# A fused decoder block on one core: three stages' weight pieces in a new order, and the weight fetches pinned in program order

## The chip, the core and the metric

The kernel runs on one core of a Trainium2 chip. The time is the device time of one execution in microseconds (us), and the median of several executions is what counts. A profile is one further execution, recorded by the hardware profiler; its own time is given beside its span. The engines are called as in the profile: PE is TensorE (PEld its weight loads), DVE is VectorE, ACT is ScalarE, POOL is GpSimd, and SP is the queue that issues most DMAs.

## What is computed

A decoder block for 256 tokens and a model width of 2048: a mixer with two branches, an output projection, a feed-forward network and a final norm, all in float32.

```python
def hybrid_mixer(h, w_in, ...):
    proj = h @ w_in                       # 16400 columns
    q, k, v, g_out, gk_low, gate_b, gate_c, xc, merge_a, merge_b = split(proj)
    log_g = log_sigmoid(gk_low @ w_gk_up + b_gk_up) / 16
    o = rmsnorm(gla_chunked(q, k, v, log_g))        # 4 heads, chunks of 64
    y_a = o * silu(g_out)
    y_b = gate_b * causal_depthwise_conv(gate_c * xc, conv_w)     # 3 taps
    return (sigmoid(merge_a) * y_a + sigmoid(merge_b) * y_b) @ w_out

h = x + hybrid_mixer(rmsnorm(x), ...)
h = h + (silu(rmsnorm(h) @ w_gate) * (rmsnorm(h) @ w_up)) @ w_down   # 5632 hidden
out = rmsnorm(h)
```

## The kernel before, in words

**Products and pieces.** All weights are read once, in pieces of 128 x 1024 values (512 KB). A piece is fetched by SP into a tile `raw` (five buffers), ACT makes its rounded upper half `hi` (`high`, L266, six buffers) and DVE the remainder `lo` (`low`, L271, five buffers). The activations are held as two such halves too. A product is three matmuls, hi by lo, lo by hi and hi by hi (`mm3`, L375 to L377). A plain piece of 512 columns has two blocks of 128 rows, for each of which it is multiplied with both halves of the tokens: twelve matmuls of 512 columns.

**Pairs.** Some column groups are computed in pairs by a scheme with seven products in place of eight (`sevens`, `seven_list`, `mixed`). A pair has 28 pieces of six matmuls. Twenty of them come in four quads q = 0 to 3, each in the order 11, t1, t3, t2, t4; then come the eight pieces 21 and 22. Sixteen pieces, the t's, are sums or differences of weight pieces that DVE makes first (`sum_of`): 11 is fetched into a tile `y` (one buffer), t1 fetches `x` (two buffers) and makes y + x into a raw tile (L287); t3, t2 and t4 then change x in place (L293), t3 and t4 with a fetched piece of their own, t2 with y. So a quad fetches y, x and two raw pieces, all by `fetch` (L260), and plain pieces are fetched at L323.

**The order.** `stream_list` writes out the order of all pieces: first k0, q0, v0; then `heads_list`, with the pair Values 2 and 3 (v2, v3) among plain pieces of other keys, queries and values; then `gates_list`, with four pairs gc and xc (the two factors ahead of the convolution) among plain pieces of the gates g, gb, ma and mb; then the output projection wo; then `hidden_list`, with pairs fg and fu among plain pieces of fg, fu and the down projection dn; then the last dn. `mixed` lays plain pieces into the gaps of a pair: one after each t, then one after each 21 and 22, and so on.

`run` takes one piece after the other. Before piece n is used, `take` has loaded all up to n + 5 (LOOK), so fetch, cast, sum and split of a piece are written down five pieces ahead of its matmuls; `low` lags one piece behind `high`. After each piece the count of ticks goes up by one, and work that was put off until then (`later`, `at`) is written down: the attention, the tables of the decay (`tables_within`, L786 and L787, at tick 22), the scores, the convolution, the merges and the transposes.

**Who orders the instructions.** The framework takes each engine's instructions in the order of the program but may move one ahead of others when it is ready sooner by its own estimate. `pin` (`keep_in_program_order`) forbids it: the instruction stays behind the one written before it on the same engine. Before the change only the convolution's and the merges' products on DVE and a few on ACT are pinned. The fetches on SP are not.

**Gates, convolution, merge.** When a gc pair is done, `conv` (one tick later) copies its product u, shifted by one and two rows, through POOL's DMA queue (L976 to L981); five pinned DVE products (L989) follow from tick CONV_AT = 12 on. `gate` finishes a plain gate; after mb it sets the merge (L994, L995) for the later of the next tick and `merge_at`, which the pair has set. The merged block is transposed (trb, L631) for wo. PSUM has eight banks; plain groups borrow theirs from the list `lent` (three banks), from which transposes, scores (sc_ps, L851) and attention products (o_ps) take one at a time.

Of the kernel before, what the change touches and what calls it, by code (L numbers as in the profile page):

```python
# [17 lines left out]
NT = T // P  # L18
D = 2048
KC = D // P  # L20
# [23 lines left out]
def plan():  # L44
# [26 lines left out]
DOWN = (WHOLE, WHOLE, WHOLE, ((0, 512), (512, 512), (1024, 512), (1536, 256), (1792, 256)))  # L71


GATES = (
    (("gc0", "xc0"), ("g1", "gb0", "mb0")),
    (("gc1", "xc1"), ("ma1", "gb1", "mb1")),
    (("gc2", "xc2"), ("g2", "ma2", "gb2")),
    (("gc3", "xc3"), ("mb2", "g3", "ma3")),
    (None, ("gb3", "mb3")),
)  # L80

# [22 lines left out]
    return [(pair, e) for e in out + list(twos)]  # L104


def mixed(pair, eights, late=None):


    if pair is None:  # L110
        return eights
    sevens = seven_list(pair)
    sums = ("t1", "t3", "t2", "t4")
    gaps = [0] * len(sevens)
    rest = len(eights)

    def deal(some, most):
        nonlocal rest
        for n, (_, e) in enumerate(sevens):
            if e[0] in some and most > 0 and rest > 0:  # L120
                gaps[n] += 1
                rest -= 1
                most -= 1

    if late is not None:
        deal(("21", "22"), late)
        while rest > 0:
            deal(sums + ("11",), rest)
    while rest > 0:
        for some in (sums, ("21", "22")):  # L130
            deal(some, rest)
    out, put = [], 0
    for e, n in zip(sevens, gaps):
        out += [e] + eights[put:put + n]
        put += n
    return out


def gates_list():
    return [e for pair, keys in GATES  # L140
            for e in mixed(pair, [(key, k) for key in keys for k in range(0, KC, 2)])]


def heads_list():


    step = {"k": 4, "q": 4, "v": 2, "g": 2, "m": 2}
    plain = [(key, k) for key in ("k1", "q1", "v1", "k2", "q2", "k3", "q3", "g0") for k in range(0, KC, step[key[0]])]
    n = plain.index(("v1", 8))
    gate = [("ma0", k) for k in range(0, KC, 2)]  # L150

    return plain[:n] + mixed(("v2", "v3"), plain[n:-1], 4) + gate[:4] + plain[-1:] + gate[4:]


def block_of(key):
# [52 lines left out]
def block_kernel(ctx, tc, x, xt, cols_in, gkw_in, gku_in, gnw, conv_w, finw, w_in, w_out, w_gu, w_dn, out):  # L208
    nc = tc.nc
    pin = tc.keep_in_program_order  # L210
    mats = {"w_in": w_in, "w_out": w_out, "w_gu": w_gu, "w_dn": w_dn}
# [40 lines left out]
    count = {"loaded": 0, "used": 0, "tick": 0}  # L252
# [4 lines left out]
    def fetch(key, k0, pool=wraw, tag="raw"):  # L257
        mat, j, n, w = index[(key, k0)]
        raw = pool.tile([P, n, w], F32, tag=tag, name=tag, bufs={"x": 2, "y": 1}.get(tag))
        nc.sync.dma_start(raw, mats[mat][j].rearrange("p (k c) -> p k c", c=w))  # L260
        return raw

    def high(raw, piece, a=0, b=None):
# [32 lines left out]
    def load_piece():  # L296


        i = count["loaded"]
        count["loaded"] += 1  # L300
        if i < len(stream):
            key, k0 = stream[i]
            if isinstance(k0, tuple):
                n, w = 2, 512
                raw = sum_of(key, *k0)
                step = n
            else:
                mat, j, n, w = index[(key, k0)]
                raw = wraw.tile([P, n, w], F32, tag="raw", name="raw")

                step = n // 2 if i < 2 else n
            piece = [whi.tile([P, n, w], F32R, tag="hi", name="hi"), None, n]
            if isinstance(k0, tuple):
                high(raw, piece)
                halfway.append((raw, piece, key, k0))
            else:
                if i < 2:
                    piece[1] = wlo.tile([P, n, w], F32R, tag="lo", name="lo")
                for a in range(0, n, step):
# [3 lines left out]
                    nc.sync.dma_start(  # L323
                        raw[:, a:b, :], mats[mat][j, :, a * w:b * w].rearrange("p (k c) -> p k c", c=w))
# [16 lines left out]
    def later(delay, fn):  # L341

        pending.append((count["tick"] + delay, fn))
# [461 lines left out]
    def at(tick, fn):  # L805
        later(tick - count["tick"], fn)
# [57 lines left out]
    o = {}  # L864
# [101 lines left out]
    us, ya, sb, merge_at = {}, {}, {}, {}  # L966

    def conv(i):
        u = us[i]
        u1 = ew.tile([P, NT, 512], F32, tag="u1", name="u1")  # L970
        u2 = ew.tile([P, NT, 512], F32, tag="u2", name="u2")
        taps = ew.tile([P, 3, 512], F32, tag="taps", name="taps")
        nc.gpsimd.dma_start(taps, conv_w[:, :, i * 512:(i + 1) * 512].to_broadcast([P, 3, 512]))
        nc.gpsimd.memset(u1[0:1, 0, :], 0.0)
        nc.gpsimd.memset(u2[0:2, 0, :], 0.0)
        nc.gpsimd.dma_start(u1[1:113, :, :], u[0:112, :, :])  # L976
        nc.gpsimd.dma_start(u2[2:114, :, :], u[0:112, :, :])
        nc.gpsimd.dma_start(u1[113:128, :, :], u[112:127, :, :])
        nc.gpsimd.dma_start(u2[114:128, :, :], u[112:126, :, :])
        nc.gpsimd.dma_start(u1[0:1, 1, :], u[127:128, 0, :])  # L980
        nc.gpsimd.dma_start(u2[0:2, 1, :], u[126:128, 0, :])  # L981

        def taps_of(j):
            return taps[:, j:j + 1, :].to_broadcast([P, NT, 512])

        for n, (dst, src, by, op) in enumerate(((u1, u1, 1, ALU.mult), (u2, u2, 0, ALU.mult), (u, u, 2, ALU.mult),
                                                (u1, u1, u2, ALU.add), (u, u, u1, ALU.add))):
            by = taps_of(by) if isinstance(by, int) else by
            later(CONV_AT + n, lambda d=dst, s=src, y=by, o=op: pin(nc.vector.tensor_tensor(out=d, in0=s, in1=y, op=o)))  # L989

    def merge(i, ts):

# [9 lines left out]
    def gated(dst, ps):  # L1002

        for t in range(NT):
            nc.scalar.activation(ps[t], ps[t], AF.Sigmoid, scale=r1[:, t:t + 1])
            nc.vector.tensor_tensor(out=dst[:, t, :], in0=dst[:, t, :], in1=ps[t], op=ALU.mult)

    def gate(key):
        i = int(key[-1])

        def done(ps):
            if key[:-1] == "g":
                ya[i] = ew.tile([P, NT, 512], F32, tag=f"ya{i % 2}", name="ya")
                for t in range(NT):
                    nc.scalar.activation(ya[i][:, t, :], ps[t], AF.Silu, scale=r1[:, t:t + 1])
# [12 lines left out]
        return done  # L1028

    def gate_pair(pair):  # L1030
        i = int(pair[0][-1])

        def second(t):
            to = us if pair[0][:-1] == "gc" else sb
            if i not in to:
                to[i] = ew.tile([P, NT, 512], F32, tag="u" if to is us else "sb", name="u" if to is us else "sb")
            return to[i][:, t, :]

        def done(t, one, two):
# [12 lines left out]

        return second, done
# [194 lines left out]
    for e in order:  # L1248
        key, k0 = e
        n = int(key.split("_")[1])  # L1250
# [80 lines left out]
```

## Time and profile before

| | before |
|---|---|
| time, median of 3 runs | 1507.15 us (1506.55 to 1508.85) |
| profiled execution: time | 1508.41 us |
| profiled execution: span | 1506.5 us |
| PE busy | 1487.1 us, 99% of the span |
| DVE busy | 1312.4 us, 87% |
| ACT busy | 874.6 us, 58% |
| read from HBM | 355.23 MB, 237 GB/s over the span |

How the views are read: a row of the timeline has the start and the length of an instruction in us, its engine, line and operation, then out<-in by the program's names; behind it in brackets stands how long the engine was idle before it and what ended that. A row of the waits has engine, tile and line of the one that waited, what it waited for, and the total in us, the number of times and the longest. A row of the windows has the stretch and its length, then the busy time and the number of instructions of PE, PEld, DVE, ACT and POOL (or of the one engine asked for), the granted clock of TensorE as a share of full speed, the DMA engines' busy share and GB/s. A row of the groups has the number of instructions, then busy us and mean ns of one, then the idle time before them. A row of the DMA issues has the queue, the number, the size of each and the median us from issue to landing. A matmul of 512 columns is shown with some 390 ns although the next one begins after 225; a stall shown as idle is therefore a little shorter than the time lost between two starts.

### The profile page before, as it was taken

What the parts mean: (1) busy time and instruction counts of PE and PEld (TensorE: products, weight loads), DVE (VectorE), ACT (ScalarE), POOL (GpSimd) and SP (SyncE); (2) the same over time, 40 slices, a digit from 0 to 9 for tenths busy, and PEclk for the clock granted to TensorE, in tenths of its full rate; (3) what the DMA queues carried; (4) which work ended last, traced back from release to release, by engine and by line L of the source; (5) the groups of instructions that cost most, each with busy time, mean ns of one, the idle gap of its engine ahead of it and who ended that gap; (6) DMA issues with size and microseconds to landing.
All of it is one profiled execution on the core that took longest, in us unless ns stands there. A gap on an engine that the chain in (4) does not pass through costs nothing.

```text
span 1506.5 us, 19393 instructions
## 1 busy us (share of the span) xinstructions
PE 1487.1 (99%) x7040; PEld 1240.7 (82%) x7040; DVE 1312.4 (87%) x1316; ACT 874.6 (58%) x990; POOL 33.0 (2%) x60
## 2 busy tenths in 40 slices
PE   9999999999999999999999999999999999999997
PEld 8979988888888788788888888888888788888887
DVE  7998878978989889976688999999999999989975
ACT  7855566655564564564566755655565556555553
POOL 0010000000001001000000000000000000000000
PEclk9999999999999999999999999999999999999999
DMA  9656677787786786787676777777877778777682
GB/s 351 216 168 193 199 238 229 238 269 234 247 294 211 242 291 225 263 296 216 210 220 220 237 257 249 250 247 232 270 240 240 258 258 273 239 265 232 229 303 87
DMA packets 101280, 362.78 MB, mean 241 GB/s; under 512 B 11620, under 2 KB 11748, under 8 KB 101056
## 3 DMA queue, kind: packets, MB, share of 16 engines
q1 hardware_dynamic: 97808, 350.92, 70.1%
q0 software_dynamic: 2800, 8.89, 2.1%
q10 hardware_dynamic: 576, 1.72, 0.3%
q8 instruction: 55, 0.90, 0.2%
q14 instruction: 41, 0.34, 0.1%
HBM read 355.23 MB, written 2.10 MB: 237 GB/s over the span
## 4 chain that ended last, share of the span: by engine, by line
PE 91%; DVE 5%; issue 1%; DMA 1%; ACT 1%; SPq 0%; DVEq 0%; ACTq 0%
PE fg L375 8%; PE fg L377 8%; PE fg L376 8%; PE dn L375 5%; PE dn L377 5%; PE dn L376 5%; PE gc L375 3%; PE gc L377 3%; PE gc L376 3%; PE wo L375 2%; PE mb L377 2%; PE mb L375 2%; PE mb L376 2%; DVE lo L271 2%; PE wo L376 2%; PE wo L377 2%
## 5 line engine op out<-in xcount | busy, mean ns | idle before, releaser
L271 DVE TENSOR_TENSOR lo<-raw,hi 128x1024 fp32r<-128x1024 f32 (+1 forms) x502 | 607.1, 1217 | 91.9 <-ACT hi L266 22.3
L266 ACT CAST hi<-raw 128x1024 fp32r<-128x1024 f32 (+1 forms) x502 | 520.0, 1047 | 242.4 <-PE mb L377 28.6
L266 ACT CAST hi<-x 128x1024 fp32r<-128x1024 f32 x156 | 164.2, 1053 | 287.4 <-DVE x L293 217.3
L271 DVE TENSOR_TENSOR lo<-x,hi 128x1024 fp32r<-128x1024 f32 x156 | 190.8, 1223 | 42.5 <-ACT hi L266 30.9
L375 PE MATMUL dn<-lo,acth 128*128 128x512 f32 (+1 forms) x368 | 140.7, 382 | 1.7 <-DVE h L1186 1.0
L377 PE MATMUL dn<-hi,acth 128*128 128x512 f32 (+1 forms) x368 | 139.9, 380 | 0.0
L376 PE MATMUL dn<-hi,actl 128*128 128x512 f32 (+1 forms) x368 | 139.8, 380 | 0.0
L293 DVE TENSOR_TENSOR x<-x,raw 128x1024 f32<-128x1024 f32 x104 | 126.8, 1219 | 12.6 <-DMA raw<-in_w_in_dram 7.8
L375 PE MATMUL fg<-lo,hh 128*128 128x512 f32 x288 | 112.4, 390 | 0.0
L377 PE MATMUL fg<-hi,hh 128*128 128x512 f32 x288 | 112.2, 390 | 0.0
L376 PE MATMUL fg<-hi,hl 128*128 128x512 f32 x288 | 112.1, 389 | 0.0
L375 PE MATMUL fg<-lo,sh 128*128 128x512 f32 x256 | 101.0, 395 | 0.0
L376 PE MATMUL fg<-hi,sl 128*128 128x512 f32 x256 | 99.9, 390 | 0.0
L377 PE MATMUL fg<-hi,sh 128*128 128x512 f32 x256 | 99.8, 390 | 0.0
L375 PEld LDWEIGHTS dn<-lo,acth 128*128 128x128 f32 x368 | 69.2, 188 | 15.8 <-DVE h L1186 1.8
L377 PEld LDWEIGHTS dn<-hi,acth 128*128 128x128 f32 x368 | 69.2, 188 | 13.3
L376 PEld LDWEIGHTS dn<-hi,actl 128*128 128x128 f32 x368 | 69.2, 188 | 12.9
L271 DVE TENSOR_TENSOR lo<-y,hi 128x1024 fp32r<-128x1024 f32 x52 | 63.4, 1219 | 4.1 <-PE g L375 1.4
L287 DVE TENSOR_TENSOR raw<-y,x 128x1024 f32<-128x1024 f32 x52 | 63.3, 1218 | 2.8 <-DMA y<-in_w_gu_dram 2.5
L293 DVE TENSOR_TENSOR x<-x,y 128x1024 f32<-128x1024 f32 x52 | 63.5, 1220 | 0.7
L375 PEld LDWEIGHTS fg<-lo,hh 128*128 128x128 f32 x288 | 54.1, 188 | 11.7 <-DVE lo L271 0.5
L377 PEld LDWEIGHTS fg<-hi,hh 128*128 128x128 f32 x288 | 54.1, 188 | 11.2
(268 smaller groups left out, 3059.4 us busy)
## 6 DMA issues: line engine op xcount, KB each, us to landing
raw<-in_w_in_dram SPq DMA_DIRECT2D x254, 512.0 KB, 4.6
raw<-in_w_gu_dram SPq DMA_DIRECT2D x176, 512.0 KB, 4.4
raw<-in_w_dn_dram SPq DMA_DIRECT2D x88, 512.0 KB, 4.5
x<-in_w_gu_dram SPq DMA_DIRECT2D x32, 512.0 KB, 5.1
y<-in_w_gu_dram SPq DMA_DIRECT2D x32, 512.0 KB, 3.9
raw<-in_w_out_dram SPq DMA_DIRECT2D x32, 512.0 KB, 3.9
y<-in_w_in_dram SPq DMA_DIRECT2D x20, 512.0 KB, 4.0
x<-in_w_in_dram SPq DMA_DIRECT2D x20, 512.0 KB, 5.1
```

The lines of the kernel that those rows point to most:

```text
L266: nc.scalar.copy(hi[:, ks, :], raw[:, ks, :])
L271: nc.vector.tensor_tensor(out=lo[:, ks, :], in0=raw[:, ks, :], in1=hi[:, ks, :].bitcast(F32), op=ALU.subtract)
L287: nc.vector.tensor_tensor(out=raw, in0=y, in1=held["x"], op=ALU.add)
L293: nc.vector.tensor_tensor(out=x, in0=x, in1=other, op=ALU.add)
L375: nc.tensor.matmul(ps, lhsT=sh, rhs=ml, start=first, stop=False, skip_group_check=onto)
L376: nc.tensor.matmul(ps, lhsT=sl, rhs=mh, start=False, stop=False, skip_group_check=onto)
L377: nc.tensor.matmul(ps, lhsT=sh, rhs=mh, start=False, stop=last, skip_group_check=onto)
```

## The change

It has three parts, and helpers for them.

1. Heads: the gaps of the pair v2 and v3 are written out as a list, HEADS. It has 25 plain pieces inside the pair in place of 27, so the pair begins two plain pieces later: behind v1's sixth piece, not its fourth. In its first quad the plain pieces behind 11, t1, t3, t2 and t4 are 2, 2, 1, 2, 1, where they were 2, 2, 2, 1, 1. At the end 1, 1, 0, 1, 0, 1, 0, 0 stand behind the 21 and 22 pieces, where it was 1, 1, 1, 1, 0, 0, 0, 0, and t1 and t4 of the last quad have none.
2. Fetches: both places that fetch weights (L260 and L323) are pinned.
3. Gates: the 14 plain gates are one list, of which each pair takes 25 pieces (before: 24, three whole gates). The second of two plain pieces comes behind t1 of the first quad. Behind the last pair 12 plain pieces are left (before 16). The last convolution's products start 7 ticks after it, not 12. As a gate can now end before or after its pair, `merge_when` is called by both, and the second call sets the merge.

```diff
-GATES = (
-    (("gc0", "xc0"), ("g1", "gb0", "mb0")),
-    (("gc1", "xc1"), ("ma1", "gb1", "mb1")),
-    (("gc2", "xc2"), ("g2", "ma2", "gb2")),
-    (("gc3", "xc3"), ("mb2", "g3", "ma3")),
-    (None, ("gb3", "mb3")),
-)
+GATES = (("gc0", "xc0"), ("gc1", "xc1"), ("gc2", "xc2"), ("gc3", "xc3"))
+GATES_PLAIN = ("g1", "gb0", "mb0", "ma1", "gb1", "mb1", "g2", "ma2", "gb2", "mb2", "g3", "ma3", "gb3", "mb3")
+GATES_EACH = 25
+
+HEADS = (2, 2, 1, 2, 1, 1, 1, 1, 1, 1, 1, 1, 1, 1, 1, 1, 0, 1, 1, 0, 1, 1, 0, 1, 0, 1, 0, 0)
...
-def mixed(pair, eights, late=None):
+def mixed(pair, eights, gaps=None):
...
+    if gaps is None:
+        gaps = [0] * len(sevens)
+        rest = len(eights)
         while rest > 0:
-            deal(sums + ("11",), rest)
-    while rest > 0:
-        for some in (sums, ("21", "22")):
-            deal(some, rest)
+            for some in (sums, ("21", "22")):
+                for n, (_, e) in enumerate(sevens):
+                    if e[0] in some and rest > 0:
+                        gaps[n] += 1
+                        rest -= 1
...
 def gates_list():
-    return [e for pair, keys in GATES
-            for e in mixed(pair, [(key, k) for key in keys for k in range(0, KC, 2)])]
+    plain = [(key, k) for key in GATES_PLAIN for k in range(0, KC, 2)]
+    out = []
+    for pair in GATES:
+        out += mixed(pair, plain[:GATES_EACH])
+        plain = plain[GATES_EACH:]
+    return out + plain
...
-    n = plain.index(("v1", 8))
+    n = len(plain) - 1 - sum(HEADS)
...
-    return plain[:n] + mixed(("v2", "v3"), plain[n:-1], 4) + gate[:4] + plain[-1:] + gate[4:]
+    return plain[:n] + mixed(("v2", "v3"), plain[n:-1], HEADS) + gate[:4] + plain[-1:] + gate[4:]
...
-        nc.sync.dma_start(raw, mats[mat][j].rearrange("p (k c) -> p k c", c=w))
+        pin(nc.sync.dma_start(raw, mats[mat][j].rearrange("p (k c) -> p k c", c=w)))
...
-                    nc.sync.dma_start(
-                        raw[:, a:b, :], mats[mat][j, :, a * w:b * w].rearrange("p (k c) -> p k c", c=w))
+                    pin(nc.sync.dma_start(
+                        raw[:, a:b, :], mats[mat][j, :, a * w:b * w].rearrange("p (k c) -> p k c", c=w)))
...
+    def merge_when(i, tick):
+
+        if i in merge_at:
+            at(max(tick, merge_at[i]), lambda: merge(i, slice(0, NT)))
+        merge_at[i] = tick
...
-                at(max(count["tick"] + 1, merge_at.get(i, 0)), lambda: merge(i, slice(0, NT)))
+                merge_when(i, count["tick"] + 1)
...
-                    merge_at[i] = count["tick"] + CONV_AT + 7
+                    merge_when(i, count["tick"] + CONV_AT[i] + 7)
...
-CONV_AT = 12
+CONV_AT = (12, 12, 12, 7)
```

More of the change, by code (lines that the diff above doesn't have):

```diff
@@ L104, in seven_list @@
     return [(pair, e) for e in out + list(twos)]
-def mixed(pair, eights, late=None):
-    if pair is None:
-        return eights
+def mixed(pair, eights, gaps=None):
     sevens = seven_list(pair)
     sums = ("t1", "t3", "t2", "t4")
[L114 to L126, printed above, removed]
-        while rest > 0:
-            deal(sums + ("11",), rest)
-    while rest > 0:
-        for some in (sums, ("21", "22")):
-            deal(some, rest)
+    if gaps is None:
+        gaps = [0] * len(sevens)
+        rest = len(eights)
+        while rest > 0:
+            for some in (sums, ("21", "22")):
[3 more added lines that the diff above has]
+                        rest -= 1
+    assert sum(gaps) == len(eights)
     out, put = [], 0
@@ L139, in gates_list @@
 def gates_list():
-    return [e for pair, keys in GATES
-            for e in mixed(pair, [(key, k) for key in keys for k in range(0, KC, 2)])]
+    plain = [(key, k) for key in GATES_PLAIN for k in range(0, KC, 2)]
[4 more added lines that the diff above has]
+    return out + plain
 def heads_list():
-    step = {"k": 4, "q": 4, "v": 2, "g": 2, "m": 2}
+    step = {"k": 4, "q": 4, "v": 2, "g": 2}
     plain = [(key, k) for key in ("k1", "q1", "v1", "k2", "q2", "k3", "q3", "g0") for k in range(0, KC, step[key[0]])]
-    n = plain.index(("v1", 8))
+    n = len(plain) - 1 - sum(HEADS)
     gate = [("ma0", k) for k in range(0, KC, 2)]
-    return plain[:n] + mixed(("v2", "v3"), plain[n:-1], 4) + gate[:4] + plain[-1:] + gate[4:]
+    return plain[:n] + mixed(("v2", "v3"), plain[n:-1], HEADS) + gate[:4] + plain[-1:] + gate[4:]
 def block_of(key):
@@ L988, in conv @@
             by = taps_of(by) if isinstance(by, int) else by
-            later(CONV_AT + n, lambda d=dst, s=src, y=by, o=op: pin(nc.vector.tensor_tensor(out=d, in0=s, in1=y, op=o)))
+            later(CONV_AT[i] + n, lambda d=dst, s=src, y=by, o=op: pin(nc.vector.tensor_tensor(out=d, in0=s, in1=y, op=o)))
     def merge(i, ts):
```

## The prediction

> **What bounds the kernel now.** I read the page first, then the waits of TensorE, then the timelines of the queues around the longest of those waits.
>
> ```profile
> span 1506.5 us, 19393 instructions
> PE 1487.1 (99%) x7040; PEld 1240.7 (82%) x7040; DVE 1312.4 (87%) x1316; ACT 874.6 (58%) x990; POOL 33.0 (2%) x60
> ```
>
> ```profile
> PE 91%; DVE 5%; issue 1%; DMA 1%; ACT 1%; SPq 0%; DVEq 0%; ACTq 0%
> ```
>
> TensorE is the bound: 99% busy, and the chain of waits runs through it for 91% of the span. The change neither adds nor removes a matmul, a split or a fetch, so it can only win or lose idle time of TensorE. The waits of TensorE say how much there is:
>
> ```profile
> PE v L375 <- DVE lo L271: 2.7, 1, 2.7
> PE ma L375 <- ACT ya L1015: 2.6, 2, 1.8
> PE warm_ps L554 <- DVE spare L550: 1.3, 1, 1.3
> PE g L375 <- DVE lo L271: 1.2, 1, 1.2
> PE dn L375 <- DVE h L1186: 1.0, 2, 0.5
> PE sc_ps L851 <- ACT o_ps L604: 0.8, 1, 0.8
> PE dn L375 <- DVE lo L271: 0.8, 1, 0.8
> PE trb L631 <- DVE sg L1145: 0.5, 1, 0.5
> PE gc L375 <- DVE lo L271: 0.5, 1, 0.5
> PE trb L631 <- DVE sb L995: 0.3, 1, 0.3
> ```
>
> The columns are total us, times, longest. Without the warm-up this is 10.4 us in three stages: heads (v, sc_ps) 3.5, gates (ma, g, gc, trb of sb) 4.6, feed-forward (dn, trb of sg) 2.3. Nearly all wait for VectorE (DVE), directly or through ScalarE (ACT). Two rates explain why. The window row below has 178 matmuls in 40 us, 0.225 us each: a plain piece (12 matmuls) feeds TensorE for 2.7 us and a piece of a pair (6) for 1.35 us. Every piece costs VectorE one split, and sixteen of a pair's 28 cost it a sum as well. Both begin some 1.13 us apart when VectorE never waits (sums at 1224.48 and 1225.61, quoted in the part on the feed-forward). Pairs starve TensorE, plain pieces restore its lead of some five pieces.
>
> ```profile
> 260.00:300.00 40.00, 40.00 (x178) 33.15 (x177) 35.73 (x31) 23.48 (x25) 0.00 (x0) 1.00 0.72 237
> ```
>
> **Heads: the pair two operands later.** The first stall stands before the pair:
>
> ```profile
> 81.18 1.53 DVE L786 TENSOR_TENSOR eq<-bc 128x512 f32<-128x512 f32 x1
> ...
> 86.03 3.21 DVE L271 TENSOR_TENSOR lo<-raw,hi 128x1024 fp32r<-128x1024 f32 x2
> ```
>
> ```profile
> 88.96 0.57 PE L375 MATMUL v<-lo,xh 128*128 128x512 f32 x1
> ...
> 92.31 0.45 PE L377 MATMUL v<-hi,xh 128*128 128x512 f32 x1
> ```
>
> ```profile
> 90.00:92.00 2.00, 2.00 (x6) 1.52 (x6) 2.00 (x3) 2.00 (x2) 0.00 (x0) 0.50 0.78 301
> ```
>
> The tables of the decay (L786, L787) hold VectorE from 81.18 to 86.03 and the split that TensorE needs comes after them. TensorE idles 2.7 us, and then its granted clock is 0.50: from 88.96 to 92.31 eight matmuls take 3.35 us instead of 1.8, so the stall costs 2.7 + 1.5 = 4.2 us. That split belongs to Values 1's third piece. Counting one piece per tick, it is the 27th of the stream, and before and after the change the first piece that differs is the 29th. Its place behind the tables is set by ticks that do not move. I book nothing here; the bounds are 0 and a gain of 4.2.
>
> The 0.8 us before the scores (sc_ps) is another matter.
>
> ```profile
> 103.16 1.05 ACT L266 CAST hi<-x 128x1024 fp32r<-128x1024 f32 x1 [2.10 <-DVE x L293]
> ```
>
> Scores of head 1 are issued one tick after the first attention product, into the same PSUM bank, and ScalarE reads that bank late because it first waits 2.10 us for a sum of the pair. Today that tick is a pair piece (1.35 us). With the pair two later it is a plain one (2.7 us), and the sum falls later than the read. The extra 1.35 us exceeds 0.8: gain 0.8. What is late next is the end of the pair, where fewer plain pieces stand between the last sums. VectorE is not full there, so I book 0 and keep 0.5 for the range.
>
> **Gates: the pinned fetches.** SP issues fetches in one queue. In program order a fetch of x stands behind the fetch of y that opens its quad. In the trace the scheduler has put x a place or more ahead:
>
> ```profile
> 474.95 0.33 SPq L260 DMA_DIRECT2D y<-in_w_in_dram  x1
> 483.44 0.33 SPq L260 DMA_DIRECT2D x<-in_w_in_dram  x1
> 483.82 1.44 SPq L323 DMA_DIRECT2D raw<-in_w_in_dram  x1
> ```
>
> ```profile
> 493.42 1.05 ACT L266 CAST hi<-raw 128x1024 fp32r<-128x1024 f32 x1 [4.30 <-DMA raw<-in_w_in_dram]
> ```
>
> ```profile
> 494.50 1.23 DVE L271 TENSOR_TENSOR lo<-raw,hi 128x1024 fp32r<-128x1024 f32 x1 [3.15 <-ACT hi L266]
> 496.03 1.22 DVE L293 TENSOR_TENSOR x<-x,raw 128x1024 f32<-128x1024 f32 x1 [0.30 <-DMA raw<-in_w_in_dram]
> ```
>
> This x belongs to the quad after that y's. It waits for one of x's two buffers, and for 8.2 us (475.3 to 483.4) SP issues nothing; the raw fetch behind it then goes out at once, so its own buffer had been free. Several raw fetches leave in a bunch, ScalarE waits 4.30 us and VectorE 3.15 + 0.30 = 3.45 us. The waits of ma, gc and trb of sb, 2.6 + 0.5 + 0.3 = 3.4 us, follow from it. Pinned, the raw fetches stand ahead of that x and go out as their buffers come free. VectorE gets 3.45 us back and TensorE its 3.4: gain 3.4, bounds 0 (VectorE late anyway, from the convolution's five products) and 3.4. What waits behind a pinned fetch is every later fetch; the only long wait in program order is y's, for the sum that frees its one buffer, and the fetches behind it are not due before it.
>
> **Gates: 25 plain pieces.** Each pair opens with two plain pieces behind its first sum instead of one: 2.7 us of TensorE for 1.13 of VectorE, 1.6 us more lead ahead of the convolution. The 1.2 us stall of g, in the last pair, is of this kind:
>
> ```profile
> 580.00:620.00 40.00, 38.80 (x175) 31.58 (x174) 39.90 (x38) 20.20 (x22) 1.84 (x3) 1.00 0.65 224
> ```
>
> VectorE is busy 39.90 of these 40 us. But x, no longer fetched early, now travels among the convolution's shift copies. I take half, 0.6, between 0 and 1.2. The tail behind the last pair shrinks from 16 plain pieces to 12, and its convolution starts seven ticks after instead of twelve. Seven plain pieces are 19 us, and the copies land within 9:
>
> ```profile
> u<-u POOLq DMA_DIRECT2D x4, 60.0 KB, 9.0
> ```
>
> Were that cover gone, the pinned product would hold every split behind it; it has some 8 us to spare. The pieces that change pairs keep their work, and the merge only waits for the later of two ends, as it did: 0.
>
> **Feed-forward: the other side of the pin.** Here x was early to its profit.
>
> ```profile
> 1216.81 0.43 SPq L260 DMA_DIRECT2D x<-in_w_gu_dram  x1
> 1221.03 0.33 SPq L260 DMA_DIRECT2D y<-in_w_gu_dram  x1
> ```
>
> ```profile
> 1224.48 1.22 DVE L293 TENSOR_TENSOR x<-x,raw 128x1024 f32<-128x1024 f32 x1
> 1225.61 1.22 DVE L287 TENSOR_TENSOR raw<-y,x 128x1024 f32<-128x1024 f32 x1
> ```
>
> ```profile
> 1238.54 1.23 DVE L271 TENSOR_TENSOR lo<-x,hi 128x1024 fp32r<-128x1024 f32 x1 [1.20 <-ACT hi L266]
> ```
>
> ```profile
> x<-in_w_gu_dram SPq DMA_DIRECT2D x32, 512.0 KB, 5.1
> y<-in_w_gu_dram SPq DMA_DIRECT2D x32, 512.0 KB, 3.9
> ```
>
> VectorE wants y and x together 4.58 us after y's issue (1225.61 less 1221.03). Pinned, x goes out 0.4 us behind y and lands 0.4 + 3.9 = 4.3 to 0.4 + 5.1 = 5.5 us after it: 0 to 0.9 us of waiting, and I take the middle, 0.45. Three such quads in each pair meet it (the first has time). Is VectorE the bound here?
>
> ```profile
> 1016.00:1200.00 184.00, 183.49 (x818) 150.89 (x817) 173.32 (x168) 102.79 (x109) 0.00 (x0) 1.00 0.77 252
> 1200.00:1345.00 145.00, 143.73 (x643) 118.38 (x642) 135.93 (x127) 84.11 (x89) 0.00 (x0) 1.00 0.77 253
> ```
>
> DVE, the third pair of numbers, is busy 94% of both stretches, and its rests are mostly like the 1.20 us above (the split of x waits for ScalarE's cast of it), so it has little left. TensorE's own rests, 0.5 and 1.3 us, come when its lead is gone. I put that at 1200, so the six quads before it (two pairs) cost 6 x 0.45 = 2.7 us in full. The later nine (4.0 us) eat a lead that grows back. Less the 0.5 us wait of trb for sg, which I put down to the one late y of the stretch (2.0 us, the row below: twenty sums, five pairs), since y then has no x ahead of it: a loss of 2.2. Bounds: a gain of 0.5 and a loss of 5.
>
> ```profile
> L287 DVE TENSOR_TENSOR raw<-y,x 128x1024 f32<-128x1024 f32 x20 | 24.3, 1217 | 2.0 <-DMA y<-in_w_gu_dram 2.0
> ```
>
> The Trainium skill, DMA: Bandwidth & Descriptors, section "Anatomy of one DMA", fits 2.0 us plus bytes at 436 GB/s. By that, y and x together (1 MB) would land in an estimated 4.4 us, inside the 4.58, and this term would be nothing and the result rival 1's. The page fits another issue path, and the medians above are longer; no row here shows such a pair alone.
>
> **The sum.** -0.8 - 3.4 - 0.6 + 2.2 = -2.6 idle, and each stall that goes also takes the drain of the matmul before it: about 0.16 us (a matmul lasts 0.39 and the next begins after 0.225). Six go (sc_ps, two of ma, gc, trb, half of g and of trb of sg): -1.0. In all -3.6. The profiled execution took 1508.41 us, 1.9 more than its span, and lies 1.3 above the median of 1507.15. So 1504.8 for that one, and 1507.15 - 3.6 = 1503.6 for the median.
>
> **Rivals.**
> 1. Larger: x is in time (the 4.3 above). Then nothing is lost in the feed-forward, and the gates give all: -0.8 - 3.4 - 1.2 - 0.5, and seven drains -1.2 = -7.1, so 1500. For it: bursts shrink when SP stops blocking. Against: the 5.1 median.
> 2. Nothing: the gates' stalls are VectorE's own, with five products, products of the gates and a merge in 20 us, and only move. Then -0.8 - 0.2 for sc_ps, a little of the rest, and 1506. For it: the 39.90 of 40 us. Against: the 3.45 us of rest ahead of 496.
> 3. Slower: in the feed-forward the scheduler, seeing x late, puts the sum of y and x behind the split of x, which must wait for ScalarE's cast, 1.20 us as at 1238.54. It decides from the point where the lead is gone: six quads ahead of 1200 count in full, 7.2 us; of the later nine's 10.8 the lead that grows back, about 8 us, swallows 8. Ten us less the 5.8 won before (0.8 + 3.4 + 0.6 + 1.0) is +4.2, so 1511.4. For it: VectorE at 94%. Against: if x is 0.9 us late the sum is still ready before the split, and then it stays where it is.
> 4. The pair's move does nothing for the opening stall: that is in the forecast. If it should go as well, 4.2 us come off any case.
>
> **How the numbers follow.** Forecast (1502 to 1505.5) 0.38, rival 1 0.20, rival 2 0.25, rival 3 0.17. A measurement here tells 0.2% (3.0 us) from no change. Three quarters of the forecast's chance and all of rival 1 are faster: 0.48. Rival 2 and the remaining quarter: 0.35. Slower: 0.17. The range goes from below rival 1, for its bounds, to between rivals 2 and 3: 1498.8 to 1509, the forecast's own being 1502 to 1505.5.
>
> **What would show it.** Right: on SP y directly ahead of its x, with no pause of 8 us in the gates; no waits of ma for ya; v's 2.7 us still there, with a clock of 0.50 behind it; sc_ps gone; sums of y and x idle some 0.5 us on DMA x in the feed-forward. Wrong: a wait of v that is gone, waits of ma that stay, or new waits of dn for lo above 3 us in all.

## The result, and the profile after

The changed kernel takes 1524.62 us (1522.79 to 1529.14, six runs) where the kernel before takes 1507.6 (six runs): a ratio of 1.0116, 95% interval 1.0101 to 1.0131. The forecast was 1503.6, so the sign was wrong: the change costs 17 us. The profiled execution took 1529.14 us; it is the slowest of the six, 4.5 us above their median. Its page:

```profile
span 1527.3 us, 19385 instructions
...
PE 1494.4 (98%) x7040; PEld 1242.4 (81%) x7040; DVE 1307.7 (86%) x1316; ACT 870.7 (57%) x990; POOL 40.2 (3%) x60
...
PE 77%; DVE 10%; DMA 5%; issue 4%; ACT 3%; POOL 1%; SPq 0%; DVEq 0%; ACTq 0%
```

TensorE has the same 7040 matmuls, but the chain of work that ended last now runs through DVE for 10% (before 5%) and through DMAs for 5% (before 1%). POOL is busy 40.2 us instead of 33.0. TensorE's waits in the changed kernel (total us, times, longest):

```profile
PE fg L366 <- DVE lo L262: 5.4, 7, 2.8
PE trb L622 <- DVE sg L1141: 4.7, 4, 2.3
PE gb L366 <- DVE ya L997: 3.2, 1, 3.2
PE o_ps L366 <- ACT sch L850: 2.6, 1, 2.6
PE ma L366 <- DVE lo L262: 1.7, 2, 1.1
PE sc_ps L844 <- ACT hi L257: 1.7, 1, 1.7
```

The waits of v, of ma for ya and of sc_ps for o_ps are gone. In their place stand waits of the feed-forward (fg, trb for sg: 10.1 us, and 1.1 of dn; dn and trb had 2.3 before), of gb in the gates (3.2) and of the scores and the first attention product in the heads (1.7 + 2.6).

The table has the length of four stages in the profiled execution of every kernel of this study, from the starts of the first matmul of gc, of wo and of fg in the timeline. The last column is the timed ratio to the kernel before. Each length comes from a single execution, and the executions of one kernel span 2.3 to 9.5 us: the profile of run 1 is its fastest of four, that of the changed kernel its slowest of six. A difference of a few us between two stages is therefore weaker evidence than a ratio. One execution of run 4 took 2128.21 us at a granted clock of 0.654 and is left out of its ratio.

| kernel | heads | gates | wo | feed-forward to end | ratio (95%) |
|---|---|---|---|---|---|
| before | 249.3 | 466.6 | 40.2 | 750.5 | 1 |
| changed | 251.6 | 469.8 | 40.6 | 765.4 | 1.0116 (1.0101 to 1.0131) |
| 1 pins alone | 251.3 | 465.7 | 43.1 | 765.7 | 1.0148 (1.0119 to 1.0176) |
| 2 changed, no pins | 250.3 | 468.0 | 40.0 | 749.9 | 1.0022 (1.0009 to 1.0036) |
| 3 heads list alone | 250.6 | 462.3 | 40.2 | 752.2 | 0.9992 (0.9978 to 1.0005) |
| 4 gates list alone | 251.2 | 469.6 | 40.0 | 750.8 | 1.0030 (1.0019 to 1.0040) |
| 5 changed, x ahead of y | 250.5 | 465.9 | 44.6 | 754.9 | 1.0059 (1.0039 to 1.0079) |
| 6 no pins, late copies | 249.3 | 469.2 | 40.0 | 752.3 | 1.0029 (1.0013 to 1.0044) |
| 7 heads list, tables on DVE | 244.0 | 465.2 | 40.2 | 751.9 | 0.9955 (0.9938 to 0.9972) |
| 8 as 5, first quads free | 250.4 | 464.1 | 40.7 | 753.9 | 0.9998 (0.9987 to 1.0009) |
| 9 old list, tables on DVE | 246.2 | 468.9 | 40.5 | 749.6 | 0.9956 (0.9942 to 0.9970) |
| 10 as 7, 25th in second quad | 244.6 | 467.7 | 40.0 | 751.7 | 0.9989 (0.9976 to 1.0001) |
| 11 as 7, mended pins in w_in | 244.3 | 462.8 | 40.2 | 751.0 | 0.9949 (0.9936 to 0.9962) |
| 12 as 8, DVE pinned too | 250.8 | 463.2 | 40.5 | 764.0 | 1.0099 (1.0083 to 1.0114) |

Some 15 of the 21 us by which the two profiled spans differ (1527.3 less 1506.5) arise in the feed-forward, where only the pins have changed anything. The costs on VectorE there are in the groups of its instructions from 762 us on (busy and mean, then the idle time before them and what ended it), first before, then changed:

```profile
L271 DVE TENSOR_TENSOR lo<-x,hi 128x1024 fp32r<-128x1024 f32 x95 | 116.2, 1223 | 26.4 <-ACT hi L266 18.9 <-PE wo L375 4.2 <-PE fg L375 0.7
L287 DVE TENSOR_TENSOR raw<-y,x 128x1024 f32<-128x1024 f32 x31 | 37.7, 1218 | 2.5 <-DMA y<-in_w_gu_dram 2.5
```

```profile
L262 DVE TENSOR_TENSOR lo<-x,hi 128x1024 fp32r<-128x1024 f32 x96 | 117.4, 1222 | 34.4 <-ACT hi L257 28.3 <-PE wo L366 4.2 <-PE fg L366 0.3
L278 DVE TENSOR_TENSOR raw<-y,x 128x1024 f32<-128x1024 f32 x31 | 37.9, 1222 | 12.9 <-DMA x<-in_w_gu_dram 12.7
```

The sum of y and x waited 2.5 us in 31 quads, for y; now it waits 12.9, for x. Of the 31 sums 16 wait, and one of them 2.57 us. The splits of x wait another 8.0 us more; the part for ScalarE's cast grew from 18.9 to 28.3. One quad in the timeline of the changed kernel, SP's queue and then VectorE:

```profile
1216.09 0.33 SPq L251 DMA_DIRECT2D y<-in_w_gu_dram  x1
1216.47 0.86 SPq L251 DMA_DIRECT2D x<-in_w_gu_dram  x1
...
1223.30 1.23 DVE L278 TENSOR_TENSOR raw<-y,x 128x1024 f32<-128x1024 f32 x1 [2.57 <-DMA x<-in_w_gu_dram]
```

x leaves 0.38 us behind y, as the pin says. Here it takes 6.7 us to land, and VectorE rests 2.57 us; TensorE's longest wait for fg, 2.8 us, is this one handed on.

In the heads the loss (2.3 us) has another face. POOL's first product of the tables across the chunks, before and changed:

```profile
80.23 1.93 POOL L796 TENSOR_TENSOR exk<-bc 128x512 f32<-128x512 f32 x1 [27.91 <-DVE bc L769]
```

```profile
80.47 9.48 POOL L787 TENSOR_TENSOR exk<-bc 128x512 f32<-128x512 f32 x1 [27.91 <-DVE bc L760]
...
81.42 0.68 DVE L777 TENSOR_TENSOR eq<-bc 128x512 f32<-128x512 f32 x1
```

Before, POOL took 1.93 us and VectorE's table beside it 1.53 (the prediction has the row). Now VectorE's takes 0.68 and POOL's 9.48. So v's split is early and its stall gone, and the tables from POOL are late: the waits of sc_ps and o_ps.

### The profile page after: what moved, and what is told of

Its sections match the earlier page's. It is cut to its first block, busy times and chain, and to the rows that moved or that the text cites. A ratio compares the mean times of both kernels' runs of the same rounds, so it can differ in the third digit from the quotient of the medians.

```text
span 1527.3 us, 19385 instructions
## 1 busy us (share of the span) xinstructions
PE 1494.4 (98%) x7040; PEld 1242.4 (81%) x7040; DVE 1307.7 (86%) x1316; ACT 870.7 (57%) x990; POOL 40.2 (3%) x60
## 4 chain that ended last, share of the span: by engine, by line
PE 77%; DVE 10%; DMA 5%; issue 4%; ACT 3%; POOL 1%; SPq 0%; DVEq 0%; ACTq 0%
PE fg L366 6%; PE fg L368 5%; PE fg L367 5%; DVE lo L262 5%; PE dn L366 4%; PE dn L367 4%; PE dn L368 4%; PE gc L366 3%; PE gc L367 3%; PE gc L368 3%; ACT hi L257 2%; DVE x L284 2%; PE gb L366 2%; PE gb L368 2%; PE gb L367 2%
## 5 line engine op out<-in xcount | busy, mean ns | idle before, releaser
L367 PEld LDWEIGHTS dn<-hi,actl 128*128 128x128 f32 x368 | 69.5, 189 | 12.9
```

Source lines behind the costliest of these rows:

```text
L367: nc.tensor.matmul(ps, lhsT=sl, rhs=mh, start=False, stop=False, skip_group_check=onto)
```

## The experiments

The theory after the result (A): the pins cost the time, since x behind y is late in nearly every quad. Its rival (B): the new lists do. They are told apart by one part at a time.

**1. The pins alone**, in the kernel before:

```diff
-        nc.sync.dma_start(raw, mats[mat][j].rearrange(...))
+        pin(nc.sync.dma_start(raw, mats[mat][j].rearrange(...)))
...
-                    nc.sync.dma_start(raw[:, a:b, :], ...)
+                    pin(nc.sync.dma_start(raw[:, a:b, :], ...))
```

> The kernel before, with the two weight fetches pinned and nothing else. Theory A (the pins make x late): x leaves behind its y at every quad, its sum with y waits for DMA x nearly every time, and the stages from the gates on lose what they lost in the changed kernel: about +15 us in the feed-forward and +3 in the gates, 1507.6 + 18 = about 1525; t1's sum (L287) idles 30 to 40 us in all, of it 20 or more on DMA x. Theory B (the new lists of heads and gates cost the time, by moving the sums into worse company): pins alone change at most what I had booked, 1503 to 1510, and L287 idles under 10 us on DMA x.

1532.95 us, ratio 1.0148: at least as dear as the whole change (the two intervals overlap), and 8 us above the 1525 I had named. The feed-forward takes 765.7, as in the changed kernel, and wo 43.1 where it took 40.2. Groups of the whole span:

```profile
L287 DVE TENSOR_TENSOR raw<-y,x 128x1024 f32<-128x1024 f32 x52 | 63.5, 1222 | 22.9 <-DMA x<-in_w_gu_dram 15.1 <-DMA x<-in_w_in_dram 7.7
```

Theory A holds for the feed-forward, though x is not late nearly every time there: 18 of the 32 sums of fg and fu wait for it. The 22.9 us are under the 30 to 40 I had named. For the gates it fails: they lose nothing by the pins (465.7 against 466.6).

**2. The changed kernel without its pins** (both lines as before the change).

> The changed kernel without its two pins: the new heads list, 25 plain pieces in the gates, the earlier last convolution. Theory A: the feed-forward stands as before (+0 to +1), the heads keep their +2.3 and the gates gain 0 to 1, so 1508 to 1511. Theory B: the loss stays, 1520 or more.

1512.22 us, ratio 1.0022, a little above the 1508 to 1511 of theory A; the feed-forward is back at 749.9, and the sums of y and x wait 1.8 us from 762 us on:

```profile
L278 DVE TENSOR_TENSOR raw<-y,x 128x1024 f32<-128x1024 f32 x31 | 37.8, 1218 | 1.8 <-DMA y<-in_w_gu_dram 1.8
```

So the pins are the whole of the feed-forward's loss, and lists without pins still cost 0.2%. The next two part these.

**3. The heads list alone** (no pins, 24 pieces, `CONV_AT = 12`).

> The kernel before with the new heads list alone. If the list decides who of POOL and VectorE is held up at the tables of the decay: POOL's first product lasts 9 us, v's stall of 2.7 us is gone, the scores and the first attention product wait 4 us together, heads +2.3 and the time about 1510. If that is chance and not the list: VectorE's tables take 1.5 us each as before, v waits 2.7 us, sc_ps does not wait, and the time is 1506.5 to 1507.6.

1508.15 us, no measurable difference. POOL's first product lasts 9.48 us here too and sc_ps and o_ps wait 1.7 + 2.6, which by my words points to the list. The next run shows that this does not follow.

**4. The gates list alone** (no pins, the old heads list):

```diff
+GATES_EACH = 25
+CONV_AT = (12, 12, 12, 7)
```

> The kernel before with 25 plain pieces in each pair of the gates and the earlier last convolution alone. Theory A: g's wait of 1.2 us shrinks, those of ma for ya stay (they hang on the fetches), 1506 to 1508. Theory B: the gates lose 3 us by the list, 1510 or more.

1513.83 us, ratio 1.0030: by the time theory B is right. The kernel with the list that was to save 0.6 us is 4.5 us slower; in the profile 3.0 of its 5.2 us stand in the gates and 1.9 in the heads. Two things are seen in the timeline. First the heads, whose instructions stand on every engine in the very order of the kernel before (compared up to 240 us):

```profile
80.01 11.82 POOL L787 TENSOR_TENSOR exk<-bc 128x512 f32<-128x512 f32 x1 [27.91 <-DVE bc L760]
```

With the same order POOL's product took 1.93 us in one execution and 11.82 in another (run 1 has 11.82 too), so it is a race that the order alone does not decide. With the new list it was late in all seven profiles that have the product on POOL; whether that list makes it likelier is not shown. Second, the gates (POOL, SP and VectorE by time):

```profile
468.90 0.58 POOL L967 DMA_DIRECT2D u<-u  x1 [75.54 <-DVE u L1037]
...
471.11 0.33 SPq L251 DMA_DIRECT2D y<-in_w_in_dram  x1
...
471.50 0.52 POOL L972 DMA_DIRECT2D u<-u  x1
...
478.06 1.23 DVE L278 TENSOR_TENSOR raw<-y,x 128x1024 f32<-128x1024 f32 x1 [2.16 <-DMA y<-in_w_in_dram]
```

The second plain piece in a pair's first quad makes the y of the second quad leave among the six shift copies of the pair before. It lands 6.9 us later, and VectorE rests 2.16 us; so it goes in three pairs (2.42, 2.16, 2.58).

**5. x directly ahead of y**, both pins kept:

```diff
         if what == "11":
+            held["x"] = fetch(two, 4 * q, held["pool"], "x")
             held["y"] = fetch(one, 4 * q, held["pool"], "y")
...
         if what == "t1":
-            held["x"] = fetch(two, 4 * q, held["pool"], "x")
```

> The changed kernel with both pins, but x fetched directly ahead of y, not behind it. Theory A1 (x behind y is the whole loss): x lands before y again, the sums L278 no longer wait for DMA x and wait for y at most as before (under 5 us in the feed-forward), and the feed-forward gets 13 to 15 us back: from the first product of fg to the end 750 to 752 us instead of 765.4; the time is at most 1.003 of the kernel before. Theory A2 (the pins cost by freezing what the scheduler had moved ahead, above all y, x and the raw pieces of a pair's first quad, and by queueing fetches behind y's wait): more than half of the loss stays, the feed-forward takes 758 or more, the ratio is 1.007 or more.

1517.2 us, ratio 1.0059: of the feed-forward's 15 us 10.5 come back (754.9). It falls between the two theories: the feed-forward halfway, the ratio nearer to A2. The sums from 762 us on wait 5.8 us, nearly all for y:

```profile
L278 DVE TENSOR_TENSOR raw<-y,x 128x1024 f32<-128x1024 f32 x31 | 37.8, 1220 | 5.8 <-DMA y<-in_w_gu_dram 5.6
```

What is left is a wo of 44.6 us, not 40.2, and 4.4 us in the feed-forward.

**6. Copies two ticks later**, without pins (`later(3, ...)` for `later(1, ...)`, `CONV_AT` less 2).

> The changed kernel without pins, its convolution's shift copies issued two ticks later (the five products keep their ticks). Theory C1 (with 25 plain pieces the y of a pair's second quad leaves in the middle of the copies of the pair before and lands 7 us later, where it took 4): y now leaves ahead of the copies, the waits of L278 for y of 2.2 to 2.6 us at some 368, 478 and 586 us shrink below 1, and the gates, from the first gc to the first wo, go from 468.0 back to 466 or less; the time is 1508 to 1510, ratio 0.999 to 1.001. Theory C2 (VectorE has simply too much to do under the new list): the gates stay at 467.5 or more, ratio 1.002.

1512.48 us, ratio 1.0029. The edit did not do what it says: POOL's queue holds nothing else, and the copies left when u was ready (466.84, y at 469.05), not at the tick. It tells nothing about the copies.

**7. The tables across the chunks on VectorE**, with the heads list alone (five lines, `nc.gpsimd` to `nc.vector`).

> The kernel before with the new heads list, and the five products of the tables across the chunks done by VectorE, not POOL. Theory D1 (the waits of the scores and of the first attention product, 1.7 + 2.6 us, come from POOL's first product, which VectorE holds up for 9.5 us): both waits go, the tables on VectorE last 0.4 to 0.7 us each whichever way, first gc comes at 246 to 248 us instead of 250.6, and the times spread less from run to run; ratio 0.997 to 0.999. Theory D2 (VectorE has no room for 3 us more there): v waits 2 to 3 us for a split again, first gc at 249 to 252, ratio 0.999 to 1.002.

1501.9 us, ratio 0.9955. D1 holds and gives more than it said: first gc at 244.0. That the times spread less is not shown: these four lie within 3.2 us, but the five of run 9, with the same tables, within 5.3, and the eleven of the kernel before that ran beside this one within 5.1. The first and the last of the five products:

```profile
86.07 0.69 DVE L787 TENSOR_TENSOR exk<-bc 128x512 f32<-128x512 f32 x1
...
88.21 0.69 DVE L791 TENSOR_TENSOR exq<-bc 128x512 f32<-128x512 f32 x1
```

Five instructions take 2.8 us in all where POOL's first alone took 9.48; neither v nor sc_ps waits, and o_ps 0.3.

**8. As 5, but y and x of a pair's first quad not pinned:**

```diff
+            hold = pin if q else (lambda ins: ins)
-            held["x"] = fetch(two, 4 * q, held["pool"], "x")
-            held["y"] = fetch(one, 4 * q, held["pool"], "y")
+            held["x"] = fetch(two, 4 * q, held["pool"], "x", hold)
+            held["y"] = fetch(one, 4 * q, held["pool"], "y", hold)
```

> As the run with x directly ahead of y, both pins, but the y and x of a pair's first quad are not pinned, so that they go out four to six fetches earlier, among the last pieces of the pair before. Theory B1 (what the pins still cost there, 4.5 us in the feed-forward and 4.4 in the output projection, is the first quads' y, which leaves among the raw pieces and lands 6 to 12 us later): the output projection takes 40 to 41 us again instead of 44.6, the feed-forward 750.5 to 752 instead of 754.9, the ratio falls from 1.006 to 1.000 to 1.002. Theory B2 (the rest comes from raw fetches held behind a waiting y): the first quads' sums no longer wait, but the two stages together get back less than 3 of the 8.9 us, and the ratio stays at 1.004 or more.

1508.7 us, ratio 0.9998. B1 is right in the ratio and in wo (40.7), and the gates gain 1.8 as well; in the feed-forward only 1.0 us comes back (753.9, not 750.5 to 752), and its sums still wait for y:

```profile
L279 DVE TENSOR_TENSOR raw<-y,x 128x1024 f32<-128x1024 f32 x31 | 37.8, 1220 | 8.3 <-DMA y<-in_w_gu_dram 8.2
```

**9. The old heads list with the tables on VectorE.**

> The kernel before with the five products of the tables across the chunks on VectorE, and the old heads list. What is left between this and the run with both is the new list alone, with POOL out of the way. If my step for the list holds (0.8 us before the scores of head 1): first gc 0.5 to 1.5 us later than that run's 244.0, with a wait of sc_ps for o_ps of some 0.8 us, and a ratio of 0.995 to 0.998. If the list only helped against POOL's lateness: first gc within 0.3 of 244.0.

1503.74 us, ratio 0.9956. First gc comes 2.15 us later than in 7, so the list is worth something without POOL, by a wait other than the one I had named:

```profile
PE sc_ps L851 <- DVE ek L840: 1.7, 1, 1.7
```

The ratio does not show it. In the profile the gates of this run took 3.7 us more than those of 7, with the same pieces in them; but the profiled execution (1506.94 us) is the slowest of five, 3.2 above their median.

**10. As 7, with 25 pieces, the 25th behind t1 of the second quad:**

```diff
+GATES_GAPS = (0, 1, 1, 1, 1, 0, 2) + (1, 1, 1) + (0, 1, 1, 1, 1) * 2 + (1,) * 8
-        out += mixed(pair, plain[:GATES_EACH])
+        out += mixed(pair, plain[:GATES_EACH], GATES_GAPS)
```

> The run with the new heads list and the tables on VectorE, with 25 plain pieces in each pair of the gates and the earlier last convolution, but the 25th piece stands behind t1 of the second quad, not of the first. Theory C1 (the 25th piece in the first quad puts the second quad's y behind the convolution's copies): y leaves before the copies and lands in some 4 us, the waits of 2.2 to 2.6 us of L278 for y go, g's wait of 1.7 us shrinks, and the gates take 463 to 465 us (465.2 with 24 pieces, 468 to 469.6 with the 25th in the first quad); ratio 0.994 to 0.996. Theory C2 (25 pieces overfill the gates wherever the 25th stands): 467 or more, ratio 0.997 or more.

1507.18 us, ratio 0.9989, 0.3% behind 7. In two of the three places y now leaves ahead of the copies (461.99 against 462.92) and is in time; at the first the sum still waits 3.65 us. But the gates take 467.7 and the ratio is above 0.997, as C2 had it. Their waits:

```profile
PE g L367 <- DVE lo L263: 1.6, 1, 1.6
...
PE trb L623 <- issue: 1.2, 1, 1.2
PE gb L367 <- DVE lo L263: 1.1, 1, 1.1
PE trb L623 <- DVE sb L987: 1.1, 1, 1.1
PE gb L367 <- DVE ya L998: 0.8, 1, 0.8
```

Most of them, g, gb and trb, stand in the run of the gates list alone too, so the late y is at most part of that list's price.

**11. As 7, with the mended pins (5 and 8) where the fetches are for w_in, and none elsewhere:**

```diff
+        if mat == "w_in" and not free:
+            pin(ins)
```

> The run with the new heads list and the tables on VectorE, to which the pins are added only where the fetches are for the first projection (heads and gates), with x ahead of y and a pair's first quad not pinned; 24 pieces per pair, feed-forward unpinned. Theory A (pins cost by x behind y and by the first quads, and where both are mended they are worth a little in the gates): the gates take 463 to 465 us (465.2 without pins), the feed-forward 750 to 752, the ratio to the kernel before 0.993 to 0.996. Rival (any pin costs): gates 467 or more, ratio 0.997 or more.

1499.91 us, ratio 0.9949: within theory A, and the rival falls, since pins on w_in with both mends cost nothing. That they gain anything is not shown: it is the fastest kernel here, but its interval overlaps with that of 7. Its gates take 462.8, its feed-forward 751.0, and of TensorE's waits these are left above 0.9 us, beside the warm-up:

```profile
PE dn L370 <- DVE h L1186: 1.9, 4, 0.8
...
PE g L370 <- DVE lo L264: 1.1, 1, 1.1
```

**12. As 8, with VectorE's sums and splits of the feed-forward pinned too.** Of the 94 to 96 splits of x from 762 us on, 16 to 19 stand directly behind their own sum under the pins, 13 without: was that the rest of the loss?

> The run with x directly ahead of y and the first quads free, 753.9 us from the first product of fg to the end, with VectorE's sums and splits of the feed-forward pinned in program order as well. Under the pins the scheduler has put 16 to 19 splits of x of the last stages directly behind the sum that makes that x (13 without pins), where VectorE must wait 1.2 us for ScalarE's cast; in program order it is 1. Theory R3 (that order is the rest of the feed-forward's loss): the idle time of L265 lo<-x in the feed-forward falls from some 30 us to under 12, and the stage takes 749 to 751 us, ratio 0.996 to 0.999. Rival (those rests are not what limits; VectorE waits elsewhere instead): the stage takes 753 or more.

1522.7 us, ratio 1.0099; the stage took 764.0. Theory R3 fell. From 762 us on:

```profile
L265 DVE TENSOR_TENSOR lo<-x,hi 128x1024 fp32r<-128x1024 f32 x94 | 115.1, 1224 | 10.8 <-ACT hi L257 5.3 <-PE wo L370 1.9
L288 DVE TENSOR_TENSOR x<-x,raw 128x1024 f32<-128x1024 f32 x63 | 77.0, 1222 | 9.2 <-DMA raw<-in_w_gu_dram 8.3
...
L1145 DVE SCALAR_TENSOR_TENSOR sg<-u,r,sg 128x512 f32<-128x512 f32 x16 | 12.0, 751 | 12.2 <-ACT sg L1142 12.0
```

The rests of the splits went from 29.6 to 10.8 us as said, and others came: VectorE now waits 12.2 us for ScalarE ahead of sg and 9.2 ahead of sums of x, 8.3 of it for raw pieces. A rest on VectorE is not worth its length by itself.

## Why the prediction was wrong

**The step that failed: the feed-forward, "so the six quads before it (two pairs) cost 6 x 0.45 = 2.7 us in full. The later nine (4.0 us) eat a lead that grows back."** The size for one quad was right on average: 12.7 us of waiting for x in 31 sums are 0.41 each, though 15 of them did not wait. The count of the quads and the lead were wrong. The gap between the two kernels can be read at the same sum in both. From the first fg to the sum at 1028.40 us of the kernel before (1036.09 now), over the first three pairs, it grows by 1.8 us; the forecast has no term for these pairs and gives no reason for leaving them out. In the next two, up to 1193.78 (1204.12 now), it grows by 2.7, which is what I had booked, in part by luck: the sums there waited 1.7 us for x. From there to the end it grows from 10.3 to 20.9 us, and there I had booked nothing. Run 1, another execution with the same pins, pays alike: 1.7, 2.3 and 11.3. Splits of x and sums of y and x in the last three pairs, before (1190 to 1409 us) and changed (1200 to 1431):

```profile
L271 DVE TENSOR_TENSOR lo<-x,hi 128x1024 fp32r<-128x1024 f32 x32 | 39.1, 1223 | 8.6 <-ACT hi L266 7.7
L287 DVE TENSOR_TENSOR raw<-y,x 128x1024 f32<-128x1024 f32 x12 | 14.6, 1217 | 2.0 <-DMA y<-in_w_gu_dram 2.0
```

```profile
L262 DVE TENSOR_TENSOR lo<-x,hi 128x1024 fp32r<-128x1024 f32 x33 | 40.3, 1222 | 13.8 <-ACT hi L257 13.4
L278 DVE TENSOR_TENSOR raw<-y,x 128x1024 f32<-128x1024 f32 x12 | 14.7, 1222 | 5.9 <-DMA x<-in_w_gu_dram 5.9
```

I had priced the lead as a store that refills and swallows the later waits; the runs give no sign of it. And the splits, which rest 5.2 us more here and 8.0 over the whole, were in rival 3 but at nothing in the forecast. Over the stage VectorE was busy 91% before (94% between 1016 and 1345), and 10.4 us more of waiting for x or y and 8.0 us more at the splits of x came out as 14.9 us of the stage. The first quads, of which I said "the first has time", did not wait at this sum in six of the eight pairs; that of the first pair of all waited 4.48 us, still in wo, and one other 0.99. Run 2 shows that the pins carry the loss, run 5 that two thirds of it is x behind y, run 8 that the first quads' head start is worth 6.7 us more over gates, wo and feed-forward. The 3.4 us that run 8 still lacks in the feed-forward stay open; in the nine profiles without pins there the stage took from 749.6 to 752.3 us, so part of it may be scatter. The order on VectorE, tried in 12, is not shown to be its cause.

Whether x could be in time was the point on which rival 1 hung. Medians from issue to landing of the changed kernel:

```profile
y<-in_w_gu_dram SPq DMA_DIRECT2D x32, 512.0 KB, 3.8
x<-in_w_gu_dram SPq DMA_DIRECT2D x32, 512.0 KB, 4.8
```

0.38 + 4.8 = 5.2 us after y's issue, where VectorE had wanted both at 4.58. The Trainium skill, DMA: Bandwidth & Descriptors, section "Anatomy of one DMA", gives by its fit, made for DMAs that GpSimd issues, an estimated 4.4 us for the two. These rows, of DMAs that SP issues, are longer, and rival 1 falls with them.

**Gates, pins: -3.4 booked, -0.9 measured** (run 1, one execution, and within the scatter below). The wait of ma for ya did shrink, from 2.6 to 0.3 us, but VectorE then waited for x, 6.4 us in the gates and 1.3 in the heads, the price that I had booked for the feed-forward alone. That the 8-us pause of SP makes the wait of ma was not borne out either: run 3 keeps the pause (476.6 to 484.8) and loses the wait. With x ahead of y and the first quads free the gates took 2.4 us less with the pins (462.8 in run 11) than without (465.2 in run 7), which is within their scatter, below.

**Gates, 25 pieces: -0.6 booked, about +3 measured.** Run 4 is 4.5 us slower, but its profile has 1.9 of that in the heads, where the order of instructions is the same. Without pins the gates took 462.3 to 468.9 us in four profiles with 24 pieces and 467.7 to 469.6 in four with 25; the means differ by 2.9. I asked what lead the piece gives and not which transfer it delays: it pushes y among the copies. Run 10 shows that this is not all of it. How the rest comes about, and what spreads the four with 24 pieces over 6.6 us, is open.

**Heads: -0.8 booked.** Where POOL is held up and nothing is pinned, the list gives 0.6 to 0.9 us (250.6 and 250.3 against 251.2). That is near the step's size, but it does not bear it out: in the profile with 251.2 the clock was halved for 6.8 us in the heads and in the other two for 3.4, and in run 6 (249.3), with the new list too, not at all. With POOL out of the way the list gave 2.15, by another wait (run 9). And v's stall of 2.7 us, whose place I said "is set by ticks that do not move", went: it hangs on who wins the race between POOL and VectorE, and run 4 shows that flip with no instruction moved. I had read one execution's stall as the kernel's.

**Rival 3** had the sign and, in the wrong place, the mechanism: it let the sum go behind a split, for +4.2. What came is VectorE resting at the sum itself, which in one quad of 31 stands directly behind a split of x; and 19 splits of x that stand directly behind their own sum, where there were 13.

## What to carry to other kernels

Before pinning a queue, look at what the scheduler has moved ahead and price each move: here it had put x ahead of y and a pair's first fetches up to a quad early, and freezing the order as written lost both; write the good order down first, then pin. None of these runs shows a clear gain from pins. A short wait that recurs can cost most of its length where the waiting engine is over 90% busy (18.4 us more of rests made 14.9 us of the stage), and a list that adds work for one engine must be read for the transfers that it delays. A stall that hangs on two engines contending should be looked at in several executions before a change is credited with it.

## What the runs showed of the hardware

A product on POOL beside VectorE's took 1.93, 8.35, 9.48 or 11.82 us, and VectorE's table 1.53 or 0.68, with the same operands. Where POOL was late, its product ended 0.9 us after VectorE's first rest: in the changed kernel at 89.95, in run 5 at 88.50, with VectorE's rests from 89.06 and 87.60, first changed, then run 5:

```profile
89.46 1.04 DVE L831 TENSOR_TENSOR eq<-eq,qr 128x512 f32<-128x512 f32 x1 [0.40 <-ACT eq L767]
```

```profile
80.15 8.35 POOL L787 TENSOR_TENSOR exk<-bc 128x512 f32<-128x512 f32 x1 [27.92 <-DVE bc L760]
...
88.34 0.71 DVE L831 TENSOR_TENSOR eq<-eq,qr 128x512 f32<-128x512 f32 x1 [0.74 <-ACT eq L767]
```

The same holds in run 4 (90.93 and 91.83), and in the kernel before POOL's product ended 0.9 us after the split at 80.07, with VectorE's next table 0.85 us longer. The Trainium skill, SBUF — State Buffer, section "SBUF: two separate sides", says of a GpSimd instruction and of certain VectorE ones, among them those with two SBUF inputs, that whichever starts first holds their common ports for the instruction and the other blocks. The rows agree in kind; that POOL stays blocked through nine to thirteen of VectorE's instructions in a row, splits among them, is what these runs add. Moving 2.8 us of work onto the busier engine shortened the heads by 6.6 us (first gc at 244.0 in run 7 against 250.6 in run 3).

TensorE's clock dropped after shorter rests than I expected. In the changed kernel the rest of 2.33 us ahead of trb (1374.81) left it at full speed, that of 2.80 ahead of fg (1225.72) halved it for some 3.4 us:

```profile
1228.00:1230.00 2.00, 2.00 (x7) 1.57 (x6) 2.00 (x2) 0.00 (x0) 0.00 (x0) 0.54 0.69 246
...
1376.00:1378.00 2.00, 2.00 (x10) 1.66 (x9) 2.00 (x3) 0.30 (x2) 0.00 (x0) 1.00 0.58 125
```

The eighth number is the granted clock. The stalls of 2.58 us (o_ps) and 3.17 us (gb) halved it too. But the length of one rest does not decide it. In run 7 a rest of 1.74 us ahead of g (601.69) was followed by a halved clock, and in run 6 one of 2.56 ahead of o_ps (104.07) was not; first run 7, then run 6:

```profile
604.00:606.00 2.00, 2.00 (x6) 1.52 (x6) 2.00 (x2) 0.54 (x1) 0.00 (x0) 0.50 0.52 209
```

```profile
106.00:108.00 2.00, 2.00 (x10) 1.64 (x9) 2.00 (x3) 1.71 (x4) 0.00 (x0) 1.00 0.85 258
```

Between 1.67 us (trb in run 12, halved) and 2.75 us (tr in run 1, not halved) both outcomes occur; what decides is not shown here.
